# The last mixer's order left to the scheduler, convolution taps at late priority, and attention scores from stacked operands

## The chip, the cores and the metric

The kernel runs on one core of one Trainium2 chip, as one launch. The metric is the device time of that core in microseconds: the median of three runs.

## The reference

Two times two transformer blocks follow each other on 512 tokens of 1024 features, in fp32. Each block is a mixer and a gated feed-forward part, each followed by a residual sum and a layer norm. The four mixers are latent attention, differential attention, a gated convolution with pooling, and the odd mixer, the last. Only the odd mixer concerns the change. It splits one projection of its input into two branches, in outline:

```python
def odd_mixer(x, w_in, forget_b, dw_w, dw_b, cn_g, cn_b, w_out):
    p = x @ w_in                       # q, k, v: 8 heads x 64; 8 forget gates; 2 x 512 for the convolution
    log_f = jax.nn.log_sigmoid(gates + forget_b)
    y_c = forgetting_attention(q, k, v, log_f)
    y_d = conformer_conv(p_conv, dw_w, dw_b, cn_g, cn_b)
    return jnp.concatenate([y_c, y_d], axis=-1) @ w_out
...
    # forgetting_attention, per block of 128 queries
    logits = q . k / sqrt(64) + cum[query] - cum[key]     # cum: running sum of log_f over the tokens
    probs = softmax(causal(logits))
    out = probs @ v
...
    # conformer_conv
    h = p[:512] * sigmoid(p[512:])
    h = causal_dwconv(h, dw_w) + dw_b  # 31 taps for each of 512 channels
    h = silu(layer_norm(h))
```

## The kernel before, in words

Every fp32 operand is held as a high part, cast to the matrix engine's format, and a low part, the difference. A product is three matrix products that add up in PSUM (`mm3`, L370: high x high, high x low, low x high). Weights come from HBM by DMAs that SyncE issues in the order of a list (`weight_plan`). Each tile of 128 rows and 1024 columns is split on arrival: ScalarE casts the high part (`whi`, L170), and VectorE or GpSimd forms the low part (`wlo`, L171). The table `ONPOOL` says which projections go to GpSimd, and `OTHERWISE` lists the tiles by number for which that is turned round.

In the odd mixer (`odd`, L1331) the projections run with the token axis as the free one, 512 columns. Two of four gated units come from the part of the program before it; units 2 and 3 (`glu`) are 48 products of 512 columns each. The values and the forget gates come from one projection of 264 columns (`W.next("od_v", 2, 264)`, 96 products), the other half of the values from `others` (48 products each for two tiles). Queries and keys come in pairs of heads (`pair`): two projections of 24 products a pair.

The convolution is a chain for each of four tiles of channels. A tap on VectorE is a product and a sum in one instruction over 128x512 elements (L1381, first taps L1379). The fourth tile's taps are a product on ScalarE into a temporary tile `tp` (L1386, two buffers) and a sum on GpSimd (L1387).

Log-sigmoid (`log_sigmoid`) is a chain of some 16 short VectorE operations on 128x32 elements with one exponential on ScalarE. `sums` makes the running sums by two products with a triangle and with ones (L1509, L1510), VectorE adds them up, ScalarE casts the high part (`cumh`, L1519), and `spread` writes high and low parts into two tiles `ab` for four heads. `rows` turns these by eight transposes (L1545); this is done for heads 0 to 3 and again for heads 4 to 7. A score block (`score`) of 128 queries is then five products: three of 64 rows (one head's features), one of four rows that adds the difference of the running sums (L1580), and one that adds the causal mask (L1581). VectorE takes the row minimum (L1593), ScalarE the exponential with its sum (L1594), VectorE the reciprocal (L1586), ScalarE the norm (L1590). The blocks are transposed (L1053), split (`pth` L1066, `ptl` L1068) and multiplied with the values (`attend`), and the output is split into `yh` and `yl` (L378, L379).

The order of all this on TensorE, VectorE, ScalarE and GpSimd is that of the code (`by_hand(Pool)`): no scheduler moves anything. `step(taps, us)` issues `us` microseconds' worth of projection products out of a list of generators (`fill`), then the vector work that the step before has left behind (`done`), then so many VectorE taps (`conv`) and GpSimd taps (`conv3`). The table `OD` says how many for each head. The order is: the gated units, the values and gates, queries and keys of the first pair with log-sigmoid and sums between them, then the heads, two deep, with the other projections as fill; then layer norm of the convolution, output projection.

Of the kernel before, what the change touches and what calls it, by code (L numbers as in the profile page):

```python
# [42 lines left out]
for _k, _w in (("g_q", 3), ("g_kv", 2), ("g_sub", 1), ("conv_w", 12), ("pool_s", 4), ("dw_w", 124),  # L43
# [11 lines left out]
OTHERWISE = (11, 12, 15, 20, 23, 24, 25, 73, 79, 80, 81, 82, 83, 84, 85, 86, 88, 90, 91, 100, 102, 103, 224, 226, 231)  # L55
# [5 lines left out]
    "taps": (0.4, 0.9, 0.7, 0.7, 0.9, 0.4, 0.2, 0.2, 1.6),  # L61
    "pool": (0.45, 0.65, 0.55, 0.45, 0.45, 0.35, 0.45, 0.35, 0.45),
    "look": (3, 2, 2, 2, 1, 1, 3, 2, 3),
    "order": 's0 s1 s2 s3 v t0 t1 t2 t3',
    "pre": (2.6, 3.4, 2.2, 2.2),
    "glu": 1.8,
    "v": 2.5,
    "pool0": 0.35,
# [169 lines left out]
def weight_plan(a):  # L238
# [53 lines left out]
    for j in range(4):  # L292
        if j < 2:
            add("od_a", a["od_d"][0, j])
        add("od_g" if j < 2 else "od_x", a["od_d"][1, j])
        if j > 1:
            add("od_x", a["od_d"][0, j])
    for u in range(4):
        add("od_v", a["od_v0"][u])
    for x in "0" + ORDER:  # L300
# [13 lines left out]
def kernel(ctx: ExitStack, tc: tile.TileContext, a: dict, out: bass.AP):  # L314
# [1016 lines left out]
    def odd(xT, open_x, FIRST, names):  # L1331
        with pool("odd") as op_:
# [16 lines left out]


            now, after, due, due3, AHEAD = [], [], [0.0], [0.0], [2]
            POOL_TAPS = [OD["pool0"]]

            def done(*work):

                after.extend(work)

            def step(taps, us=0.0):
                fill.take(us)
                work = list(now)  # L1360
                now[:], after[:] = after, []
                for w in work:
                    w()
                if W.at < W.used + AHEAD[0]:
                    W.prep()
                due[0] += taps
                n = int(due[0])
                due[0] -= n
                conv(n)
                due3[0] += POOL_TAPS[0]  # L1370
                n = int(due3[0])
                due3[0] -= n
                conv3(n)

            def tap(j, k, pool=False):
# [8 lines left out]
                else:  # L1384
                    tp = op_.tile([P, S], F32, name="tp", tag="tp", bufs=2)
# [3 lines left out]
            TAPS = [deque((j, k) for k in range(CONV)) for j in range(4)]  # L1389
            GL, turn_of = set(), deque(range(3))  # L1390

            def conv(n):

                while n > 0:
                    for j in (*turn_of, 3):
                        if j in GL and TAPS[j]:
                            break
                    else:
                        return
                    tap(*TAPS[j].popleft())  # L1400
                    if j < 3:
                        turn_of.remove(j)
                        turn_of.append(j)
                    n -= 1

            def conv3(n):

                while n > 0 and 3 in GL and TAPS[3]:
                    tap(*TAPS[3].popleft(), pool=True)
                    n -= 1  # L1410

            def gate(j, pa, pg):
                nc.scalar.activation(cv[j], pg, AF.Sigmoid)
                nc.vector.tensor_mul(gl[j][:, CONV - 1:], cv[j], pa)
                GL.add(j)
# [7 lines left out]
            def glu(j):  # L1423
                pg = acc()
                yield from steps_T(pg, "od_x")
                done(lambda: nc.scalar.activation(cv[j], pg, AF.Sigmoid))
                pa = acc()
                yield from steps_T(pa, "od_x")

                def times():  # L1430
                    nc.vector.tensor_mul(gl[j][:, CONV - 1:], cv[j], pa)
                    GL.add(j)

                done(times)

            Q, MADE, SCORED = {}, set(), set()

            def pair(p):
                got = []
                while p > 1 and 2 * p - 3 not in SCORED:  # L1440
                    yield None
                for s in range(2):
                    ps = acc()
                    yield from steps_T(ps, ("od_q", "od_k")[s])
                    hi = ov.tile([P, S], F32R, name="qh", tag=f"qh{s}", bufs=2)
                    lo = ov.tile([P, S], F32R, name="ql", tag=f"ql{s}", bufs=2)
                    got += [hi, lo]
                    done(lambda hi=hi, lo=lo, ps=ps, s=s: split(hi, lo, ps, -0.125 if s == 0 else None))
                done(lambda: Q.update({p: got}))
# [19 lines left out]
            def have(p):  # L1469
                fill.until(lambda: p in Q or p in MADE)  # L1470
                while p not in Q:
                    step(1)

            fill = Fill([glu(2), glu(3)])
# [4 lines left out]
            while fill.parts:  # L1479
                step(OD["glu"], 1.3)  # L1480
            fill.parts.extend([pair(0)] + [others() if x == 'v' else pair(int(x)) for x in ORDER])
# [6 lines left out]
            def log_sigmoid():  # L1488
# [4 lines left out]
                conv(2)  # L1493
# [3 lines left out]
                conv(1)  # L1497
# [7 lines left out]
            def sums():  # L1505
# [6 lines left out]
                def add():  # L1512
# [7 lines left out]
                    spread(0)  # L1520
# [7 lines left out]
            ab = [op_.tile([P, NT, 4, 32], F32, name=f"ab{i}", tag=("yh", "yl")[i], bufs=4) for i in range(2)]  # L1528
            for i in range(2):
                nc.gpsimd.memset(ab[i], 0.0)  # L1530
                nc.gpsimd.memset(ab[i][:, :, :, 2 * i:2 * i + 2], 1.0)
            AB = {}

            def spread(g):
                c, h = cum[:, :, 4 * g:4 * g + 4], f32(cumh[:, :, 4 * g:4 * g + 4])
                nc.vector.tensor_copy(ab[1][:, :, :, 0], h)
                nc.vector.tensor_sub(ab[1][:, :, :, 1], c, h)
# [353 lines left out]
```

## Time and profile before

| what | value |
|---|---|
| median of three runs | 2274.2 us (2273.18, 2274.2, 2282.26) |
| profiled execution | 2284.52 us, its span 2282.7 us |
| mean granted clock of TensorE | 0.988 of full speed |
| busy over the whole span | TensorE 97%, VectorE 76%, ScalarE 44%, GpSimd 11% |
| odd mixer's first row minimum (start) | 1748.00 us |
| last head's low half `yl` (start) | 1871.57 us |
| first output product with a convolution half (start) | 1893.96 us |

Times in the rows are from the start of the span. The share of an engine over the whole span says little about the odd mixer, which is a tenth of it; the windows further down cut its stretches out. Durations of successive instructions of an engine overlap a little, so that the distance of their starts is the cost of one in a run of many. TensorE's granted clock stands as a share of its full 2.4 GHz; 0.50 is 1.2 GHz.

### The profile page before, as it was taken

How to read it: one execution, taken by the hardware profiler on the slowest of the kernel's cores; microseconds unless marked ns; L12 is line 12 of the kernel's file. 1: busy time of each engine (PE TensorE's matmuls, PEld its weight loads, DVE VectorE, ACT ScalarE, POOL GpSimd, SP SyncE). 2: the span in 40 equal slices, each digit the busy share in tenths (PEclk: the TensorE clock that was granted, in tenths of full speed). 3: DMA queues.
4: the chain of work that ended last, by engine and by line, in shares of the span. 5: the costliest groups of instructions: out<-in, count | busy, mean ns of one | idle time of the engine just before them, and what ended most of it. 6: DMA issues, size and time to landing. Idle time of an engine off the chain costs nothing. (4 is left out here: it accounts for less than half of the span.)

```text
span 2282.7 us, 35239 instructions
## 1 busy us (share of the span) xinstructions
PE 2223.8 (97%) x14148; PEld 1987.0 (87%) x14148; DVE 1729.6 (76%) x2806; ACT 994.5 (44%) x1665; POOL 246.6 (11%) x195
## 2 busy tenths in 40 slices
PE   8999999999999999999999999999998999999997
PEld 8888999998987789999988899999886768999996
DVE  5777888886666788888675688887766756988886
ACT  4655444433665454433342344343325654443341
POOL 2200000001312100000000000000046521000001
PEclk9999999999999999999999999999998979999999
DMA  5213333333221133233232333333222013333331
GB/s 172 64 47 102 102 112 97 98 93 105 96 67 65 37 120 111 94 111 103 92 107 93 100 104 111 103 93 111 65 88 83 28 38 108 96 107 106 103 100 57
DMA packets 59364, 210.50 MB, mean 92 GB/s; under 512 B 6624, under 2 KB 6880, under 8 KB 59200
## 3 DMA queue, kind: packets, MB, share of 16 engines
q1 hardware_dynamic: 56304, 198.97, 27.7%
q0 software_dynamic: 2320, 8.23, 1.2%
q8 instruction: 111, 1.82, 0.3%
q10 hardware_dynamic: 576, 1.05, 0.1%
q14 instruction: 53, 0.43, 0.1%
HBM read 206.12 MB, written 2.10 MB: 91 GB/s over the span
## 5 line engine op out<-in xcount | busy, mean ns | idle before, releaser
L170 ACT ACTIVATE whi<-wraw 128x1024 fp32r<-128x1024 f32 (+3 forms) x528 | 520.0, 988 | 814.0 <-PE acc L372 481.8
L171 DVE TENSOR_TENSOR wlo<-wraw,whi 128x1024 fp32r<-128x1024 f32 (+2 forms) x475 | 536.8, 1131 | 117.0 <-ACT whi L170 116.0
L371 PE MATMUL acc<-xh,whi 128*128 128x256 f32 (+1 forms) x1712 | 527.7, 308 | 0.4 <-DVE kl L1098 0.4
L372 PE MATMUL acc<-xl,whi 128*128 128x256 f32 (+1 forms) x1712 | 523.7, 306 | 3.1 <-DVE xl L481 3.1
L373 PE MATMUL acc<-xh,wlo 128*128 128x256 f32 (+1 forms) x1712 | 522.9, 306 | 2.9 <-DVE wlo L171 2.9
L372 PEld LDWEIGHTS acc<-xl,whi 128*128 128x128 f32 x1712 | 323.6, 189 | 27.6 <-DVE xl L481 4.3
L371 PEld LDWEIGHTS acc<-xh,whi 128*128 128x128 f32 x1712 | 323.6, 189 | 24.7 <-DVE kl L1098 0.5
L373 PE MATMUL acc<-xs,wlo 128*128 128x256 f32 x1216 | 341.3, 282 | 0.0
L372 PE MATMUL acc<-xql,whi 128*128 128x256 f32 x1216 | 341.0, 281 | 0.0
L373 PEld LDWEIGHTS acc<-xh,wlo 128*128 128x128 f32 x1712 | 323.2, 189 | 19.5 <-DVE wlo L171 3.9
L371 PE MATMUL acc<-xs,whi 128*128 128x256 f32 x1216 | 339.0, 280 | 0.0
L372 PEld LDWEIGHTS acc<-xql,whi 128*128 128x128 f32 x1216 | 228.5, 188 | 5.5
L371 PEld LDWEIGHTS acc<-xs,whi 128*128 128x128 f32 x1216 | 229.6, 189 | 3.5
L373 PEld LDWEIGHTS acc<-xs,wlo 128*128 128x128 f32 x1216 | 228.1, 188 | 0.3
L171 POOL TENSOR_TENSOR wlo<-wraw,whi 128x1024 fp32r<-128x1024 f32 (+2 forms) x53 | 130.4, 2463 | 548.0 <-ACT whi L170 547.6
L389 POOL TENSOR_TENSOR lnr<-lnv,mhalf 128x1 f32<-128x1 f32 x32 | 23.7, 740 | 1264.4 <-DVE lnv L387 1264.4
L371 PE MATMUL tr<-whi,hh 128*128 128x512 f32 (+1 forms) x296 | 117.8, 398 | 0.0
L782 DVE TENSOR_TENSOR sums<-sums,acc 128x512 f32<-128x512 f32 x76 | 52.2, 687 | 85.5 <-PE acc L373 85.0
L372 PE MATMUL tr<-wlo,hh 128*128 128x512 f32 (+1 forms) x296 | 116.8, 395 | 0.0
L373 PE MATMUL tr<-whi,hl 128*128 128x512 f32 (+1 forms) x296 | 115.8, 391 | 0.0
L373 PE MATMUL ps<-whi,hl 128*128 128x512 f32 x288 | 113.7, 395 | 0.0
L371 PE MATMUL ps<-whi,hh 128*128 128x512 f32 x288 | 113.4, 394 | 0.0
(355 smaller groups left out, 4140.5 us busy)
## 6 DMA issues: line engine op xcount, KB each, us to landing
wraw<-in_gu_dram SPq DMA_DIRECT2D x176, 512.0 KB, 3.6
wraw<-in_dn_dram SPq DMA_DIRECT2D x88, 512.0 KB, 3.5
wraw<-in_ev_in_dram SPq DMA_DIRECT2D x16, 512.0 KB, 3.6
wraw<-in_mla_o_dram SPq DMA_DIRECT2D x8, 512.0 KB, 3.7
wraw<-in_df_q_dram SPq DMA_DIRECT2D x8, 512.0 KB, 3.5
wraw<-in_df_k_dram SPq DMA_DIRECT2D x8, 512.0 KB, 3.6
wraw<-in_df_v_dram SPq DMA_DIRECT2D x8, 512.0 KB, 3.6
wraw<-in_df_o_dram SPq DMA_DIRECT2D x8, 512.0 KB, 3.6
```

The lines of the kernel that those rows point to most:

```text
L170: self.nc.scalar.activation(hi, raw[:, o:o + n], AF.Copy)
L171: eng.tensor_sub(lo, raw[:, o:o + n], hi.bitcast(F32))
L371: nc.tensor.matmul(ps, ah, bh, start=first, stop=False)
L372: nc.tensor.matmul(ps, ah, bl, start=False, stop=False)
L373: nc.tensor.matmul(ps, al, bh, start=False, stop=last)
L389: nc.gpsimd.tensor_tensor(r[:, :n], v[:, :n], mhalf[:, :n], op=OP.pow)
L782: nc.vector.tensor_add(g[:, 1:3], g[:, 1:3], v)
```

## The change

The region in which the code's order holds is gone for the odd mixer: the scheduler orders the instructions of all engines by priorities and its own costs. `done` runs its work at once, `step` only issues fill, and the quotas of taps are gone. When a gated unit is there, all 31 taps of its tile are issued with a priority that lies 4000 and more behind (`conv`).

The value and gate projection comes ahead of the gated units 2 and 3 (the weights' list too). The log sums are taken at the sixth step of those units and the bias rows made at the ninth, for all eight heads at once. `tp` has one buffer.

The scores' operands are stacked in tiles of 128 rows, two heads a pair, two pairs in turn: `qa` holds a head's high query part and the bias rows, `qq` its high and low parts, `kb` the high key part and the bias (chosen for the head by `own_rows`), `kk` the low and the high one. A block is two products of 128 rows and the mask.

```diff
-OTHERWISE = (..., 224, 226, 231)
+OTHERWISE = (..., 224, 226, 227)
...
+    "sums": 6,
+    "rows": 9,
+    "late": 4000,
...
             def done(*work):
-
-                after.extend(work)
-
-            def step(taps, us=0.0):
-                fill.take(us)
-                work = list(now)
-                now[:], after[:] = after, []
                 for w in work:
                     w()
+
+            def step(us=0.0):
+                fill.take(us)
                 if W.at < W.used + AHEAD[0]:
                     W.prep()
-                due[0] += taps
...
-                    tp = op_.tile([P, S], F32, name="tp", tag="tp", bufs=2)
+                    tp = op_.tile([P, S], F32, name="tp", tag="tp", bufs=1)
...
+            def conv(j):
+
+                at = tc.cur_priority
+                for k in range(CONV):
+                    tc.cur_priority = at + OD["late"] + 20 * k + 4 * j
+                    tap(j, k, j == 3)
+                tc.cur_priority = at
...
+            STACK = [[[ov.tile([P, S], F32R, name=f"{n}{b}{m}") for n in ("qa", "qq", "kb", "kk")]
+                      for m in range(2)] for b in range(2)]
...
+            def place(p, s, ps):
+
+                every = [(*STACK[p % 2][m], HALF[m], HALF[1 - m]) for m in range(2)]
+                for qa, qq, kb, kk, own, other in every:
+                    nc.scalar.activation((kb if s else qq)[own], ps[own], AF.Copy, scale=1.0 if s else -0.125)
+                for qa, qq, kb, kk, own, other in every:
+                    if s:
+                        nc.vector.tensor_sub(kk[own], ps[own], f32(kb[own]))
+                    else:
+                        nc.vector.scalar_tensor_tensor(qq[other], ps[own], -0.125, f32(qq[own]), op0=OP.mult, op1=OP.subtract)
+                for qa, qq, kb, kk, own, other in every:
+                    nc.scalar.activation(kk[other] if s else qa[own], f32((kb if s else qq)[own]), AF.Copy)
+
+            def bias(p):
+
+                for m in range(2):
+                    h, other = 2 * p + m, HALF[1 - m]
+                    nc.scalar.activation(STACK[p % 2][m][2][other], f32(ROWS["k"][other]), AF.Copy, scale=own_rows[other, h:h + 1])
...
-            region = ExitStack()
-            region.enter_context(by_hand(mybir.EngineType.Pool))
...
-                qh, ql, kh, kl = Q[p]
-                ms = slice(64 * i, 64 * i + 64)
+                qa, qq, kb, kk = Q[h // 2][h % 2]
...
-                mm3(ps[:, :n], qh[ms, qs], ql[ms, qs], kh[ms, :n], kl[ms, :n], True, False)
-                r = slice(32 * (h % 4), 32 * (h % 4) + 4)
-                nc.tensor.matmul(ps[:, :n], AB[h // 4, 0][r, qs], AB[h // 4, 1][r, :n], start=False, stop=False)
+                nc.tensor.matmul(ps[:, :n], qa[:, qs], kb[:, :n], start=True, stop=False)
+                nc.tensor.matmul(ps[:, :n], qq[:, qs], kk[:, :n], start=False, stop=False)
                 nc.tensor.matmul(ps[:, qs], idb, mkb, start=False, stop=True)
...
+            fill.parts.extend([glu(2), glu(3)])
+            n = 0
+            while fill.parts:
+                step(1.3)
+                n += 1
+                if n == 1:
+                    choose()
+                if n == OD["sums"]:
+                    sums()
+                if n == OD["rows"]:
+                    rows()
```

VectorE, in the log-sigmoid (`lf` are its tiles, `cv` the convolution's sums, `gl` the gated units, `sm` the taps' weights); first before, then after:

```order
L1494 TENSOR_SCALAR lf_17226<-lf_17226 128x32
L1495 RECIPROCAL lf_17226<-lf_17226 128x32
L1496 TENSOR_TENSOR lf_17226<-lf_17226 128x32
L1381 SCALAR_TENSOR_TENSOR cv1_17060<-gl1_17056,sm_91,cv1_17060 128x512
L1498 TENSOR_TENSOR lf_17226<-lf_17226 128x32
L1499 TENSOR_SCALAR lf_17226<-lf_17226 128x32
L1501 SCALAR_TENSOR_TENSOR lf_17226<-lf_17226 128x32 x8
L1502 SCALAR_TENSOR_TENSOR lf_17226<-lf_17226 128x32
L1503 SCALAR_TENSOR_TENSOR lf_17226<-lf_17226 128x32
L1381 SCALAR_TENSOR_TENSOR cv2_17061<-gl2_17057,sm_91,cv2_17061 128x512
L1381 SCALAR_TENSOR_TENSOR cv0_17059<-gl0_17055,sm_91,cv0_17059 128x512
```

```order
L1473 RECIPROCAL lf_17151<-lf_17151 128x32
L1363 SCALAR_TENSOR_TENSOR cv0_17059<-gl0_17055,sm_91,cv0_17059 128x512
L1363 SCALAR_TENSOR_TENSOR cv1_17060<-gl1_17056,sm_91,cv1_17060 128x512
L1474 TENSOR_TENSOR lf_17151<-lf_17151 128x32
L1363 SCALAR_TENSOR_TENSOR cv0_17059<-gl0_17055,sm_91,cv0_17059 128x512
L1363 SCALAR_TENSOR_TENSOR cv1_17060<-gl1_17056,sm_91,cv1_17060 128x512
L1475 TENSOR_TENSOR lf_17151<-lf_17151 128x32
L1363 SCALAR_TENSOR_TENSOR cv0_17059<-gl0_17055,sm_91,cv0_17059 128x512
L1363 SCALAR_TENSOR_TENSOR cv1_17060<-gl1_17056,sm_91,cv1_17060 128x512
L1476 TENSOR_SCALAR lf_17151<-lf_17151 128x32
L1381 TENSOR_TENSOR gl2_17057<-cv2_17061,acc_17341 128x512
```

Eleven rows of before hold the log-sigmoid up to its last step but for three taps and one low half of the queries; eleven rows of after hold four of its steps (one reciprocal ahead, two products, one sum) with six taps and a gated unit between them.

TensorE at head 0's first score blocks (`ps` the score banks, `acc` the projections', `rows` the bias rows, `mkb` and `idb` the mask); first before, then after:

```order
L371 MATMUL ps_17538<-qh_17480,qh_17437 128x128
L372 MATMUL ps_17538<-ql_17481,qh_17437 128x128
L373 MATMUL ps_17538<-qh_17480,ql_17438 128x128
L1580 MATMUL ps_17538<-rows_17520,rows_17514 128x128
L1581 LDWEIGHTS idb_17051
L1581 MATMUL ps_17538<-mkb_17053,idb_17051 128x128
L371 MATMUL acc_17482<-xh_16571,whi_17423 128x512
L372 MATMUL acc_17482<-xl_16572,whi_17423 128x512
L373 MATMUL acc_17482<-xh_16571,wlo_17424 128x512
L371 MATMUL ps_17559<-qh_17480,qh_17437 128x256
```

```order
L369 MATMUL acc_18067<-xl_16572,whi_17754 128x512
L370 MATMUL acc_18067<-xh_16571,wlo_17755 128x512
L1569 MATMUL ps_17678<-kb00_17069,qa00_17067 128x128
L1570 MATMUL ps_17678<-kk00_17070,qq00_17068 128x128
L1571 LDWEIGHTS idb_17051
L1571 MATMUL ps_17678<-mkb_17053,idb_17051 128x128
L1569 MATMUL ps_17700<-kb00_17069,qa00_17067 128x256
L1570 MATMUL ps_17700<-kk00_17070,qq00_17068 128x256
L1571 LDWEIGHTS idb_17051
L1571 MATMUL ps_17700<-mkb_17053,idb_17051 128x128
```

The block is five products and then three, and a projection (`acc`) stood between two blocks of before where after the blocks follow each other.

ScalarE at the cast of the log sums' high part (`cumh`; `tp` is the fourth convolution tile's product, `qh` and `kb`, `kk` high parts of queries and keys); first before, then after:

```order
L170 ACTIVATE whi_17423<-wraw_17362 128x1024
L170 ACTIVATE whi_17448<-wraw_17421 128x1024
L1386 ACTIVATE tp_17453<-gl3_17058,sm_91 128x512
L381 ACTIVATE qh_17437<-acc_17373 128x512
L1519 ACTIVATE cumh_17227<-lf_17226 128x32
L170 ACTIVATE whi_17498<-wraw_17446 128x1024
```

```order
L1368 ACTIVATE tp_17519<-gl3_17058,sm_91 128x512
L167 ACTIVATE whi_18073<-wraw_17837 128x1024
L1410 ACTIVATE kb10_17077<-acc_17748 64x512
L1410 ACTIVATE kb11_17081<-acc_17748 64x512
L1368 ACTIVATE tp_17522<-gl3_17058,sm_91 128x512
L1496 ACTIVATE cumh_17152<-lf_17151 128x32
L1417 ACTIVATE kk10_17078<-kb10_17077 64x512
```

Before, one convolution product stands two rows ahead of the cast, with two buffers to go to; after, one stands right ahead of it, with one buffer, which the 20th GpSimd instruction of the mixer (a sum `cv3` of the product before) leaves free.

## Rows read from the trace of the kernel before

**Rows 1.** Windows: length; busy of PE, PEld, DVE, ACT, POOL; clock; DMA share; GB/s.
```profile
1677.70:1748.00 70.30, 59.04 (x289) 48.90 (x287) 57.25 (x95) 19.39 (x30) 34.03 (x18) 0.90 0.24 70
1748.00:1871.60 123.60, 119.68 (x570) 88.80 (x570) 84.43 (x171) 84.07 (x198) 63.01 (x35) 0.88 0.13 37
```

**Rows 2.** Windows within the attention heads.
```profile
1760.00:1840.00 80.00, 78.55 (x409) 58.92 (x408) 60.60 (x118) 55.83 (x132) 45.14 (x27) 0.96 0.09 27
1840.00:1860.00 20.00, 19.51 (x57) 13.31 (x57) 8.72 (x23) 11.52 (x31) 6.48 (x4) 0.50 0.28 79
```

**Rows 3.** Timeline of TensorE: start us, us, instruction, [idle before <-releaser].
```profile
1731.91 0.61 PE L1509 MATMUL ps<-lf,cst 128*128 128x32 f32 x2 [7.82 <-issue]
```

**Rows 4.** Waits, 1677.7 to 1894: total us, times, longest us.
```profile
ACT e L1594 <- DVE sums L1593: 24.2, 15, 5.1
```

**Rows 5.** Timeline of VectorE in the first stretch.
```profile
1679.09 3.07 DVE L1379 TENSOR_SCALAR cv<-gl,sm 128x512 f32<-128x512 f32 x2
...
1704.59 6.70 DVE L1381 SCALAR_TENSOR_TENSOR cv<-gl,sm,cv 128x512 f32<-128x512 f32 x10
...
1719.83 0.42 DVE L379 TENSOR_TENSOR vl<-ps,vh 128x256 fp32r<-128x256 f32 x1 [0.45 <-ACT vh L378]
```

**Rows 6.** Timeline of GpSimd in the first stretch.
```profile
1679.48 2.40 POOL L171 TENSOR_TENSOR wlo<-wraw,whi 128x1024 fp32r<-128x1024 f32 x1 [3.83 <-ACT whi L170]
...
1706.13 8.67 POOL L171 TENSOR_TENSOR wlo<-wraw,whi 128x528 fp32r<-128x528 f32 x2 [8.57 <-ACT whi L170]
...
1719.46 1.29 POOL L1387 TENSOR_TENSOR cv<-cv,tp 128x512 f32<-128x512 f32 x1
```

**Rows 7.** Timeline of TensorE: score products of heads 0, 6 and 7.
```profile
1749.10 0.50 PE L371 MATMUL ps<-qh 64*128 64x512 f32 x1
...
1750.42 0.23 PE L1581 MATMUL ps<-mkb,idb 128*128 128x128 bf16 x1
...
1835.92 0.32 PE L371 MATMUL ps<-qh 64*128 64x128 f32 x1
...
1847.57 0.47 PE L371 MATMUL ps<-qh 64*128 64x128 f32 x1
```

**Rows 8.** Lines of ScalarE, 1748 to 1871.6: count, busy us, mean ns, idle before.
```profile
L1386 ACT ACTIVATE tp<-gl,sm 128x512 f32<-128x512 f32 x26 | 18.8, 722 | 0.0
L1590 ACT ACTIVATE e<-e,sums 128x128 f32<-128x128 f32 (+3 forms) x32 | 17.9, 559 | 7.5 <-DVE sums L1586 7.5
L1594 ACT ACTIVATE e<-ps,sums 128x128 f32<-128x128 f32 (+3 forms) x32 | 16.8, 525 | 24.2 <-DVE sums L1593 24.2
L1066 ACT ACTIVATE pth<-tr 128x256 fp32r<-128x256 f32 (+1 forms) x48 | 14.2, 350 | 5.4 <-PE tr L1053 5.0
L170 ACT ACTIVATE whi<-wraw 128x1024 fp32r<-128x1024 f32 x9 | 9.5, 1057 | 0.0
L1594 ACT ACTIVATION_READ_ACCUMULATOR e<-ps,sums 128x1 f32 x32 | 6.2, 193 | 0.0
L378 ACT ACTIVATE yh<-ps 64x512 fp32r<-64x512 f32 x8 | 4.7, 590 | 5.8 <-PE ps L373 5.6
```

**Rows 9.** Timeline of ScalarE, an accumulator and what follows.
```profile
1749.69 0.19 ACT L1594 ACTIVATION_READ_ACCUMULATOR e<-ps,sums 128x1 f32 x1
1749.79 0.71 ACT L1386 ACTIVATE tp<-gl,sm 128x512 f32<-128x512 f32 x1
```

**Rows 10.** Timelines of VectorE and TensorE at the ends of the stretches.
```profile
1748.00 0.28 DVE L1593 TENSOR_REDUCE sums<-ps 128x1 f32<-128x128 f32 x1
1748.80 0.17 DVE L1586 RECIPROCAL sums<-sums 128x1 f32<-128x1 f32 x1 [0.53 <-ACT e L1594]
...
1871.57 0.69 DVE L379 TENSOR_TENSOR yl<-ps,yh 64x512 fp32r<-64x512 f32 x1
...
1893.72 0.39 PE L373 MATMUL acc<-whi,yl 128*128 128x512 f32 x1
1893.96 0.39 PE L371 MATMUL acc<-whi,vh 128*128 128x512 f32 x1
```

More of the change, by code (lines that the diff above doesn't have):

```diff
@@ L291, in weight_plan @@
     ffn("2", 0)
[L292 to L297, printed above, removed]
+    for j in range(2):
+        add("od_a", a["od_d"][0, j])
+        add("od_g", a["od_d"][1, j])
     for u in range(4):
         add("od_v", a["od_v0"][u])
+    for j in range(2, 4):
+        add("od_x", a["od_d"][1, j])
+        add("od_x", a["od_d"][0, j])
     for x in "0" + ORDER:
@@ L1444, in pair @@
                     yield from steps_T(ps, ("od_q", "od_k")[s])
[L1445 to L1449, printed above, removed]
+                    done(lambda ps=ps, s=s: place(p, s, ps))
+                if p:
+                    done(lambda: bias(p))
+                done(lambda: Q.update({p: STACK[p % 2]}))
                 MADE.add(p)
@@ L1470, in have @@
                 fill.until(lambda: p in Q or p in MADE)
-                while p not in Q:
-                    step(1)
-            fill = Fill([glu(2), glu(3)])
-            region = ExitStack()
-            region.enter_context(by_hand(mybir.EngineType.Pool))
+                assert p in Q
+            fill = Fill([])
             for j in range(2):
                 gate(j, *FIRST[2 * j:2 * j + 2])
-            while fill.parts:
-                step(OD["glu"], 1.3)
-            fill.parts.extend([pair(0)] + [others() if x == 'v' else pair(int(x)) for x in ORDER])
             vh = op_.tile([P, NT, S], F32R, name="vh")
@@ L1548, in rows, with put @@
-                if g == 0:
-                    done(lambda: spread(1))
+                        nc.tensor.transpose(got[i][:, t * P:(t + 1) * P], ab[i][:, t].rearrange("p d h r -> p (d h r)"), ident)
+                def put():
+                    ROWS["k"] = op_.tile([P, S], F32R, name="rows", tag="yh", bufs=4)
+                    nc.scalar.activation(ROWS["k"], got[1], AF.Copy)
+                    for b in range(2):
+                        for m in range(2):
+                            other = HALF[1 - m]
+                            nc.scalar.activation(STACK[b][m][0][other], got[0][other], AF.Copy)
+                        if b == 0:
+                            bias(0)
@@ L1551, in value @@
+                done(put)
             def value(t, ps):
@@ L1594, in soft @@
                     nc.scalar.activation(e, ps[:, :n], AF.Exp, bias=sums[:, 0:1], scale=-1.0, accum_out=sums[:, 1:2])
-                    now.insert(0, norm)
-                done(soft)
+                    norm()
+                soft()
             def turn_e(h, qb):
@@ L1637, in out_w @@
                 return lambda kc: [w[:, kc % 2] for w in OUT[c][kc // 2]]
-            step(1, OD["pre"][0])
-            step(1, OD["pre"][1])
-            sums()
-            step(1, OD["pre"][2])
-            step(1, OD["pre"][3])
+            fill.parts.extend([glu(2), glu(3)])
[9 more added lines that the diff above has]
+                    rows()
+            fill.parts.extend([pair(0)] + [others() if x == 'v' else pair(int(x)) for x in ORDER])
+            while 0 not in MADE:
+                step(1.3)
             have(0)
@@ L1646, in odd @@
             turns.update(acc=turns["acc"][2:], ps=turns["ps"] + turns["acc"][:1], tr=turns["tr"] + turns["acc"][1:2])
-            rows(0)
-            step(1, 1.0)
-            step(1, 1.0)
             C, OUT = [], {}
             for h in range(-1, 8):
-                us, n, POOL_TAPS[0] = (OD[k][h + 1] for k in ("fill", "taps", "pool"))
+                us = OD["fill"][h + 1]
                 AHEAD[0] = OD["look"][h + 1]
```

99 lines of the change are left out of this document (29 added, 70 removed).

## The prediction

> **What bounds the kernel now.** I read the busy times of the last mixer's stretches first [rows 1]: from the end of the first two gated units' projections to the first row minimum of the softmax, and from there to the last head's low half. A third, from there to the first output product that takes a convolution half, ends at 1893.96 [rows 10]. These 216.3 us are all that the change touches: the instructions ahead of 1677.7 us and behind 1893.96 are the same. The middle stretch is TensorE's: 119.7 of 123.6 us busy, and in its best part, the 80 us of [rows 2], TensorE is at 78.6, VectorE at 60.6, ScalarE at 55.8. In the first stretch it is busy 59.0 of 70.3 us and VectorE 57.3: no engine fills it.
>
> The granted clock comes next. It is 0.90 over the first stretch and 0.88 over the middle one [rows 1], 0.50 from 1840 to 1860 [rows 2], where the heads have no projection beside them. At 0.10 of 70.3 and 0.12 of 123.6 some 20 us go to the lower level, and 16 us to idling, the longest 7.8 us ahead of the log-sum product [rows 3]. Some 178 us are work at the full level.
>
> Then the list of waits. The largest that matters is ScalarE's 24.2 us for row minima [rows 4], which themselves wait for TensorE's scores. So in the middle stretch a shorter score block pays at once. In the first stretch what ends last is the chain of gates, log-sigmoid, log sums, bias rows and scores.
>
> Last, single rows of VectorE and GpSimd [rows 5, 6]. Two first taps, 0.5 us each elsewhere, take 3.07 together while GpSimd's low half of 1024 columns runs its 2.40. Ten taps from 1704.59 take 6.70, and of GpSimd's two halves from 1706.13 the first came through only when they were done. From 1679.1 to the end of those ten, 1711.3, VectorE's ten rows hold 37 taps at 0.66, three first taps, two gates and a low half, 27.8 us. GpSimd's three halves in it are 2.40 and, at 528 columns, twice 1.24: 4.9. The sum is 32.7, the stretch 32.2. Instructions with both operands in SBUF run one at a time on these two engines. Against that, GpSimd's tap sum at 1719.46 took 1.29 beside a value half of VectorE at 1719.83 that reads PSUM and took 0.42: no delay to either.
>
> By the Trainium skill (SBUF — State Buffer, "Who interferes with whom") an instruction of VectorE with two SBUF inputs and one of GpSimd that reads SBUF lock each other out for a whole instruction, and one with a single SBUF input does not. The trace agrees with both halves, except that GpSimd's half at 1706.13 was left out through several taps, not one. By the page, the PSUM readers below come off the sum; were it wrong there, the sum below would be 9.3 us longer.
>
> **The change part by part.**
>
> *Scores.* A block had five products (three of 64 rows, one of 4, the mask) and now has three. The four blocks of head 0 took 0.76, 0.90, 1.12 and 1.36 us, 4.14 together; the last runs from 1749.10 to just behind the mask at 1750.42 [rows 7]. Two of five products less is 1.66 us a head. If products of 128 rows follow each other as the output's do (0.24 us for 512 columns [rows 10], half for 256), a head would take some 1.9 and save 2.2. I take 1.6: 13 us for eight heads where TensorE bounds, double at half clock.
>
> *Stacked operands.* For each pair there are 8 half-row casts and copies, and 2 more for the bias, on ScalarE, about 0.59 us each by the 64x512 row [rows 8], and 4 half-row differences on VectorE, 0.69 each [rows 10]. They replace two casts and two differences of 128 rows. ScalarE gets some 24 operations more in all, 14 us. In the first stretch it has room (19.4 of 70.3 busy), in the middle it counts.
>
> *Order of VectorE's work.* This is the largest term. Before, log-sigmoid stands nearly alone, log sums and spread follow, and taps fill what is left. Now VectorE has 75 of its 93 taps between the first gate and the last write of the bias rows, one to three between any two steps of the log-sigmoid. 75 x 0.66 (the row of ten: 0.67) is 49.5. Readers of PSUM: three gates at 0.69, four value halves at 0.42, eight half-row differences at 0.69, 9.3. The 31 small operations (log-sigmoid, sums, spread) at 0.13, somewhat under the reciprocal's 0.17 [rows 10]: 4.0. Together 62.8 us.
>
> *GpSimd.* ScalarE's cast of the log sums stands behind a convolution product that needs the one temporary buffer left (two before). So GpSimd must be through 20 instructions first: 12 low halves of 1024 columns at 2.40 are 28.8, one of 528 at 1.24, 7 tap sums at 1.29 are 9.0: 39.0 us. Locked out of each other the two make 62.8 + 39.0 - 9.3 = 92.5 us, and 101.8 with no overlap. From 1677.7 the bias rows are written at 1770 to 1779. Without any lock it would be 1740.5, VectorE alone.
>
> *Behind it.* TensorE's projections up to there are 96 products of 264 columns, 192 of 512 and 66 of 256, some 64 us at full clock. It is through with them by about 1745, and stands ahead of the log sums and again ahead of the rows, 10 to 15 us each. What is queued behind its wait: 8 transposes (1 us), 30 products of 0.12 and 24 of 0.24, 9.1 us at full clock and 18 at half, then the first scores, for which VectorE, ScalarE and in the end everything waits. VectorE has 14 taps and two value halves ahead of the first minimum, 10.6 us, and about 5 of GpSimd's lie between. First minimum at 1785 (1776 to 1792), where it was 1748.00 [rows 10]: +37 us (+28 to +44).
>
> *Heads.* With most projections behind it the middle stretch holds less for TensorE. Without a fill beside it a head came 11.65 us behind another at half clock (1835.92 to 1847.57 [rows 7]). Less 3.3 for the scores that is 8.35, times 8 is 67; the three projections of queries and keys left in it (72 products of 0.24) are 16.8 us at full clock, 34 at half: 84 to 101. ScalarE cannot go under its own sum, by the rows of the middle stretch [rows 8]: exponentials 16.8, their accumulators 6.2, norms 17.9, transposed copies 14.2, output halves 4.7, 18 tap products at 0.72, 4 weight halves at 1.06, 20 half-row copies at 0.59, 88.8 in all. An instruction there starts 0.1 us before the one ahead of it ends (1749.69 and its 0.19, then 1749.79 [rows 9]); with that off for some 170 of them it is 72. I take 91 us, between 84 and 101, for heads without fill are the nearest rows. Before it was 123.6: -33 (-52 to -23).
>
> *End.* From the last head's low half to the first convolution product it was 22.4 us [rows 10]. The work stays, some output parts have been issued ahead: -1 (-3 to +2).
>
> *Weights.* The value weights come four loads earlier on SP's queue, the gate weights later, and one low half goes to VectorE in place of another. The DMA share is 0.24 and 0.13 [rows 1]: at nothing, hidden by the 11.7 us of value products ahead. With that cover gone it is one low half, 2.4 us.
>
> **Sum.** +37 - 33 - 1 = +3 us on the profiled execution's 2284.5. That one lies 10.3 above the runs' median of 2274.2; from the median, 2277.
>
> **The rivals.**
>
> *Faster A: the first stretch is not bound by one port.* For it: GpSimd's 63.0 us and VectorE's 84.4 went into the 123.6 of the middle stretch, so there is some overlap. Against it: the 32.7 in 32.2 above. The rows would be written at 1740 to 1745, the first minimum come at about 1757 (+9), the heads as above: 9 - 33 - 1 = -25, so 2249.
>
> *Faster B: the heads run at ScalarE's pace.* First minimum at its early bound (+28), the middle at 78 (72 and a start), -46, the end -1: -19, so 2255. For it: at full clock TensorE would need about 34 + 17 = 51 us there. Against it: heads without fill have been granted 0.50 [rows 2].
>
> *Slower: TensorE drops to its lower level ahead of the bias rows and stays there.* With no overlap the rows are written at 1779, TensorE has stood for 25 us or more, its 9.1 us take 18, the first minimum comes at 1792 (+44), the heads take 101 (-23): +21, so 2295. It decides from where VectorE and GpSimd need over 98 us together. For it: the 32.7 in 32.2. Against it: the 1.29 of the tap sum at 1719.46.
>
> *The change doesn't do what it says.* Taps at late priority would stand behind the log sums. By the order 75 of them stand ahead; the forecast has that already.
>
> **How the numbers follow.** A measurement of this kernel can tell 0.5%, 11.4 us, from no change, so the borders are 2262.8 and 2285.6. Forecast 0.42 (its own range 2264 to 2290), slower rival 0.28, faster A 0.12, faster B 0.18. Of the forecast a tenth ends above 2285.6, and a little of faster B above 2262.8: faster 0.29, same 0.39, slower 0.32. The range reaches a little past faster A and the slower rival: 2247 to 2302.
>
> **What would show it.** Right: the first row minimum at 1776 to 1792; TensorE idle for 20 us or more ahead of the bias rows' transposes while VectorE and GpSimd take turns; score blocks of 512 columns under 0.85 us at full clock; heads 9 to 12 us apart. Wrong: a first minimum before 1765 (the port term), heads 15 us apart (TensorE no lighter), or under 9 (ScalarE's pace).

## The result, and the profile after

The changed kernel takes 2293.1 us (median of 6 runs, 2291.1 to 2294.5), the kernel before 2274.6 beside it: a ratio of 1.0071 (1.0052 to 1.0089). It is slower by 18.5 us by these medians, and by 12 to 20 us by the interval of the ratio.

All 70 runs of before on record spread from 2273 to 2285 us, with a median of 2278.2; the six of the change lie within 3.4 us. A second profile of before (the first experiment) shows where two executions of it part, and its stretches are given beside those of the rows.

| stretch | before, shown execution | before, second profile | after |
|---|---|---|---|
| 1677.7 to the first row minimum | 70.3 | 69.4 | 116.3 |
| to the last head's `yl` | 123.6 | 113.8 | 89.0 |
| to the first convolution product | 22.4 | 23.7 | 17.9 |
| first convolution product, start | 1893.96 | 1884.62 | 1900.86 |
| span | 2282.7 | 2273.2 | 2291.3 |

The windows of after answer to [rows 1] and have its columns; the first stretch is cut where the bias rows are written:

```profile
1677.70:1773.70 96.00, 70.78 (x365) 60.10 (x364) 95.50 (x121) 36.84 (x52) 48.02 (x23) 0.84 0.25 77
1773.70:1794.00 20.30, 12.48 (x75) 10.87 (x74) 19.99 (x18) 12.01 (x17) 13.29 (x6) 0.88 0.25 78
1794.00:1883.00 89.00, 74.73 (x384) 58.34 (x384) 49.82 (x138) 76.16 (x194) 32.46 (x22) 0.89 0.06 19
1883.00:1900.90 17.90, 15.95 (x80) 12.86 (x78) 11.11 (x18) 6.13 (x8) 5.82 (x3) 1.00 0.20 63
```

VectorE is busy for 95.5 of the 96.0 us to the bias rows, with GpSimd at 48.0 beside it; TensorE has 70.8. In the heads TensorE fell from 119.7 to 74.7 and ScalarE has the most, 76.2 of 89.0. Two short windows of after, one in either part:

```profile
1740.00:1750.00 10.00, 0.00 (x0) 0.00 (x0) 9.93 (x9) 8.10 (x13) 9.17 (x6) 0.50 0.32 105
1850.00:1860.00 10.00, 9.31 (x58) 7.43 (x58) 6.38 (x20) 9.95 (x29) 3.08 (x4) 1.00 0.00 0
```

In the first TensorE does nothing, its clock is granted at 0.50, and VectorE and GpSimd are both "busy" nearly all the time. In the second the clock is 1.00 and ScalarE has no time left; so it is from 1830 to 1870 (39.6 of 40 us), but not over the whole of the heads (76.2 of 89.0).

TensorE's timeline of after, the product of the log sums, the queries behind the bias rows, a score block of 512 columns, the first convolution product (to be read against [rows 3, 7 and 10]):

```profile
1755.40 0.61 PE L1486 MATMUL ps<-lf,cst 128*128 128x32 f32 x2 [19.71 <-issue]
...
1792.67 0.79 PE L368 MATMUL acc<-xh,whi 128*128 128x512 f32 x1 [7.82 <-DVE vl L376]
...
1847.88 0.48 PE L1569 MATMUL ps<-kb,qa 128*128 128x512 f32 x1
1848.19 0.40 PE L1570 MATMUL ps<-kk,qq 128*128 128x512 f32 x1
1848.43 0.23 PE L1571 MATMUL ps<-mkb,idb 128*128 128x128 bf16 x1
...
1900.86 0.50 PE L368 MATMUL acc<-whi,vh 128*128 128x512 f32 x1 [1.96 <-ACT vh L375]
```

The 7.8 us wait ahead of the log sums has become 19.7, and there is a second one of 7.8 us, for a value half on VectorE. The score block takes 0.59 us, from 1847.88 to 0.04 behind the start of its mask, where that of [rows 7] takes 1.36 by the same count. The products of before between the two rows shown there are

```profile
1749.43 0.40 PE L372 MATMUL ps<-ql,qh 64*128 64x512 f32 x1
1749.67 0.39 PE L373 MATMUL ps<-qh,ql 64*128 64x512 f32 x1
1750.00 0.49 PE L1580 MATMUL ps<-rows 4*128 4x512 f32 x1
```

VectorE's timeline of after, which answers to [rows 5 and 10]: a step of the log-sigmoid, three taps, the last write of the bias rows, the taps in front of a value half, the first minimum, the last `yl`:

```profile
1706.27 2.38 DVE L1472 TENSOR_SCALAR lf<-lf 128x32 f32<-128x32 f32 x1
...
1737.86 7.30 DVE L1363 SCALAR_TENSOR_TENSOR cv<-gl,sm,cv 128x512 f32<-128x512 f32 x3
...
1773.45 0.27 DVE L1523 TENSOR_TENSOR ab<-cumh,lf 128x64 f32<-128x64 f32 x1
...
1777.33 14.69 DVE L1363 SCALAR_TENSOR_TENSOR cv<-gl,sm,cv 128x512 f32<-128x512 f32 x9
1791.93 0.68 DVE L376 TENSOR_TENSOR vl<-acc,vh 128x512 fp32r<-128x512 f32 x1
...
1793.98 0.62 DVE L1583 TENSOR_REDUCE sums<-ps 128x1 f32<-128x128 f32 x2
...
1882.96 0.69 DVE L376 TENSOR_TENSOR yl<-ps,yh 64x512 fp32r<-64x512 f32 x1
```

GpSimd's timeline of after at the first two of them, which answers to [rows 6]:

```profile
1705.99 2.63 POOL L168 TENSOR_TENSOR wlo<-wraw,whi 128x1024 fp32r<-128x1024 f32 x1 [1.95 <-ACT whi L167]
...
1737.86 2.35 POOL L168 TENSOR_TENSOR wlo<-wraw,whi 128x1024 fp32r<-128x1024 f32 x1
1740.16 1.71 POOL L1369 TENSOR_TENSOR cv<-cv,tp 128x512 f32<-128x512 f32 x1
1741.83 2.79 POOL L168 TENSOR_TENSOR wlo<-wraw,whi 128x1024 fp32r<-128x1024 f32 x1
```

Three taps (2.0 us alone) take 7.30 beside two low halves and a tap sum. The step at 1706.27 works on 32 columns and takes 2.38 us: it ends with GpSimd's half, which began 0.28 us before it. The mean tap up to the bias rows is 1067 ns, where ten in a row took 0.67 each [rows 5]:

```profile
L1363 DVE SCALAR_TENSOR_TENSOR cv<-gl,sm,cv 128x512 f32<-128x512 f32 x73 | 75.1, 1067 | 0.3
```

### The profile page after: what moved, and what is told of

It is laid out like the page before. It is cut to its first block, busy times and chain, and to the rows that moved or that the text cites. A ratio compares the mean times of both kernels' runs of the same rounds, so it can differ in the third digit from the quotient of the medians.

```text
span 2291.3 us, 35147 instructions
## 1 busy us (share of the span) xinstructions
PE 2198.8 (96%) x14076; PEld 1974.9 (86%) x14076; DVE 1755.5 (77%) x2813; ACT 1016.7 (44%) x1700; POOL 239.2 (10%) x195
## 5 line engine op out<-in xcount | busy, mean ns | idle before, releaser
L167 ACT ACTIVATE whi<-wraw 128x1024 fp32r<-128x1024 f32 (+2 forms) x528 | 520.8, 989 | 833.4 <-PE acc L369 513.0
L368 PE MATMUL acc<-xh,whi 128*128 128x256 f32 (+1 forms) x1712 | 527.6, 308 | 14.9 <-DVE vl L376 7.8
L386 POOL TENSOR_TENSOR lnr<-lnv,mhalf 128x1 f32<-128x1 f32 x32 | 23.7, 740 | 1271.2 <-DVE lnv L384 1271.1
```

What stands on the lines that cost most here:

```text
L167: self.nc.scalar.activation(hi, raw[:, o:o + n], AF.Copy)
L368: nc.tensor.matmul(ps, ah, bh, start=first, stop=False)
L386: nc.gpsimd.tensor_tensor(r[:, :n], v[:, :n], mhalf[:, :n], op=OP.pow)
```

## The experiments

**The kernel before again**, unchanged.

> The kernel before once more, unchanged, for a second profile of it: its runs fall into two groups, about 2274 and about 2283, and the trace shown is one of the upper group. If the upper group is a matter of the odd mixer's clock, a profile of the lower group shows the same instruction order with a granted clock above 0.88 in the heads (1748 to 1872) and the first convolution product some 9 us earlier than 1893.96. Rival: the difference lies ahead of the odd mixer (before 1677 us), and the mixer's stretches are the same 70.3, 123.6 and 22.4 us.

2274.97 us. Its windows of the heads, and of the 20 us that [rows 2] show:

```profile
1747.10:1860.90 113.80, 109.63 (x570) 81.69 (x570) 84.21 (x171) 83.66 (x198) 62.99 (x35) 0.97 0.14 41
1840.00:1860.00 20.00, 18.07 (x91) 13.09 (x90) 13.06 (x28) 13.49 (x31) 4.95 (x3) 0.95 0.21 56
```

and the first convolution product:

```profile
1884.62 0.40 PE L371 MATMUL acc<-whi,vh 128*128 128x512 f32 x1
```

The order is the same, the clock is 0.97 over the heads and 0.95 where it was 0.50, and the product comes 9.3 us earlier. The two executions are 9.5 us apart in all, and their heads 9.8 (123.6 and 113.8). So the execution on which the prediction's terms rest had inside its heads nearly all of the 10.3 us that lie between it and the median of three. What decides which clock an execution gets was not found.

**One port or a long queue.** GpSimd writes zeros where it formed the low halves of the odd mixer's projections (a part of the result is left out):

```diff
-        eng.tensor_sub(lo, raw[:, o:o + n], hi.bitcast(F32))
+        if eng is self.nc.gpsimd and self.plan[self.at - 1][0] in ("od_x", "od_v", "od_q", "od_k"):
+            eng.memset(lo.bitcast(F32), 0.0)
+        else:
+            eng.tensor_sub(lo, raw[:, o:o + n], hi.bitcast(F32))
```

> The changed kernel, with GpSimd writing zeros in place of the low halves of the odd mixer's projections: a part of the computation is left out, the instruction only writes and reads nothing. It tells the port from VectorE's own queue. One port: the 13 halves of 2.4 us no longer stand in VectorE's way, the bias rows (1773.7) come at 1744 to 1752, where 76 taps and the 62.8 us of VectorE with GpSimd's 9 us of tap sums end, and the time falls by 20 us or more, to 2265 to 2275. Rival, VectorE's queue: the rows stay at 1770 or later and the time above 2285.

2259.7 us (two runs), 0.9928 (0.9907 to 0.9949) of before. GpSimd's lines up to the bias rows, and the last write of them on VectorE:

```profile
L1372 POOL TENSOR_TENSOR cv<-cv,tp 128x512 f32<-128x512 f32 x10 | 15.5, 1550 | 9.4 <-ACT tp L1371 9.4
L169 POOL MEMSET wlo<- 128x1024 f32 x13 | 12.4, 956 | 32.5 <-PE acc L373 24.7 <-PE ps L373 5.9 <-PE ps L372 1.8
```

```profile
1745.64 0.27 DVE L1526 TENSOR_TENSOR ab<-cumh,lf 128x64 f32<-128x64 f32 x1
```

Nine taps in a row, and the two operations of GpSimd that ran beside them:

```profile
1682.62 6.05 DVE L1366 SCALAR_TENSOR_TENSOR cv<-gl,sm,cv 128x512 f32<-128x512 f32 x9
...
1683.87 0.95 POOL L169 MEMSET wlo<- 128x1024 f32 x1 [2.02 <-PE ps L373]
1686.78 0.95 POOL L169 MEMSET wlo<- 128x1024 f32 x1 [1.96 <-PE ps L373]
```

Each tap took 0.67, as alone [rows 5]: an operation that only writes did not hold them up. 76 taps stand ahead of the rows (75 in the change), and these come at 1745.9 in place of 1773.7. The thirteen halves that read thus cost VectorE 28 us, some 2.1 each, with VectorE's queue nearly as it was: the time goes to the port, by which the expectation means that the two engines lock each other out, and not to the length of the queue. The first minimum comes at 1761.9, 32 us earlier, and the time falls by 33, to less than the 2265 to 2275 that were expected. The zeros also go into TensorE's products; what that does to the time was not told apart, but TensorE does not set the rows, for VectorE is busy for 67.4 of the 68.2 us up to them.

**The low halves on VectorE.**

```diff
-ONPOOL = ("od_x", "od_v", "od_q", "od_k", "od_o", "uq_n", "ukv", "df_o", "mla_o")
+ONPOOL = ("od_o", "uq_n", "ukv", "df_o", "mla_o")
-OTHERWISE = (..., 224, 226, 227)
+OTHERWISE = (..., 224, 226)
```

> The changed kernel, with the low halves of the odd mixer's projections on VectorE in place of GpSimd: 13 operations that cost GpSimd 2.4 us cost VectorE about 1.15. One port (my theory): VectorE gets 15 us more and GpSimd 30 us less, their sum falls by 15, so the bias rows are written near 1760 where they were at 1773.6, the first row minimum comes 10 to 15 us earlier than 1794, the time is 2280 to 2285. Rival, VectorE's own queue is what is long: the rows are written some 14 us later, near 1787, and the time is 2303 or more.

2276.6 us, 0.9990 (0.9980 to 0.9999): 16.5 us off the change by giving work to the busier engine. VectorE's lines up to the bias rows:

```profile
L1363 DVE SCALAR_TENSOR_TENSOR cv<-gl,sm,cv 128x512 f32<-128x512 f32 x70 | 61.3, 904 | 0.2
L168 DVE TENSOR_TENSOR wlo<-wraw,whi 128x1024 fp32r<-128x1024 f32 x14 | 18.1, 1291 | 0.1
```

The taps fall from 1067 to 904 ns. The rows came at 1772.0, hardly earlier, against the expectation: the scheduler now put 16 of GpSimd's tap sums ahead where there were 9, and VectorE has 18 us of halves. The first minimum came at 1779.1, 14.9 us earlier: both value halves that stand ahead of it were done by 1764, where in the change they start at 1776.7 and 1791.9:

```profile
1763.28 0.68 DVE L376 TENSOR_TENSOR vl<-acc,vh 128x512 fp32r<-128x512 f32 x1
...
1771.69 0.26 DVE L1523 TENSOR_TENSOR ab<-cumh,lf 128x64 f32<-128x64 f32 x1
...
1779.12 0.28 DVE L1583 TENSOR_REDUCE sums<-ps 128x1 f32<-128x128 f32 x1
```

So the first minimum gained what was expected, in another place, and the time fell by more than the 8 to 13 us that were expected.

**Taps held behind the log sums.** Taps from the 13th on of tiles 0 and 1, and all of tile 2, are queued behind the last spread:

```diff
+                    if SPREAD:
+                        with tc.issue_after(SPREAD[0]):
+                            tap(j, k, j == 3)
+                    else:
+                        tap(j, k, j == 3)
...
-                conv(j)
+                if j == 3 or SPREAD:
+                    conv(j)
+                else:
+                    conv(j, 0, 12)
+                    GATED.append(j)
```

> The changed kernel, with all taps but the first 12 of the tiles 0 and 1 queued behind the spread of the log sums on VectorE: 24 taps ahead of the bias rows in place of 75. If the taps ahead are what makes the rows late, 51 x 0.66 = 34 us go: rows near 1740, the gap before the log sums (19.7 us) gone, first minimum near 1770 (33 taps now lie between rows and first minimum), and since ScalarE rather than VectorE bounds the heads, most of the 24 us stay: 2270 to 2278. Rival, only moved: the taps come back ahead of the first minimum and in the heads (36 there in place of 4), where VectorE and GpSimd exclude each other again, and the time stays at 2288 to 2294.

2277.6 us, 1.0003 (0.9992 to 1.0014), 15.5 us off the change. Rows at 1715.7, 58 us earlier where 34 were expected; first minimum at 1754.9, 39 us earlier; the heads then took 113.0, 24 longer:

```profile
1715.39 0.26 DVE L1533 TENSOR_TENSOR ab<-cumh,lf 128x64 f32<-128x64 f32 x1
```

```profile
1754.90:1867.90 113.00, 95.46 (x526) 76.23 (x526) 91.03 (x175) 88.94 (x212) 55.29 (x33) 0.95 0.11 33
```

VectorE's 91 and GpSimd's 55 us are there now. The taps' place decides the rows, as expected, but three fifths of the first minimum's gain are given back in the heads: the time is in the expected range, and the rival was right on where the taps go.

**Both**, as two edits together.

> Both remedies on the changed kernel: all taps but 24 queued behind the spread of the log sums, and the projections' low halves on VectorE. If each takes away another part of what the port costs, the first minimum comes near 1748 and the heads grow less than with held taps alone (113 us), to about 100: 2260 to 2270, under both kernels. Rival, the work of VectorE is only moved about, 50 taps now lie beside the heads: 2272 to 2280, no better than either remedy.

2265.5 us, 0.9942 (0.9926 to 0.9958): faster than both kernels. The last write of the rows, the first minimum, and the windows about it:

```profile
1716.38 0.27 DVE L1533 TENSOR_TENSOR ab<-cumh,lf 128x64 f32<-128x64 f32 x1
...
1738.34 0.29 DVE L1596 TENSOR_REDUCE sums<-ps 128x1 f32<-128x128 f32 x1
```

```profile
1677.70:1738.30 60.60, 55.88 (x289) 47.30 (x288) 54.78 (x94) 37.02 (x52) 8.87 (x6) 0.96 0.33 105
1738.30:1856.30 118.00, 96.17 (x525) 77.44 (x524) 104.66 (x192) 88.28 (x210) 52.88 (x30) 0.93 0.11 36
```

GpSimd has 8.9 us of the first stretch. The first minimum comes 10 us earlier than was expected, and the heads take 118.0 where about 100 were: they are longer, not shorter, than with held taps alone, and 50 taps are among them where there were 36. With 36 taps ahead of the spread in place of 24:

> The fastest version so far (2265.5) with 36 taps ahead of the log sums' spread in place of 24, so 41 in place of 50 behind the first minimum. Its bias rows were written at 1716.7 and its first minimum came at 1738.3, so 8 us more ahead of the rows should cost nothing there and take 6 us from the heads (118 us long): 2258 to 2264. Rival, the first minimum moves by as much as the heads shorten: 2264 to 2269.

2265.7 us, 0.9941 (0.9919 to 0.9963), no gain: the rows went from 1716.7 to 1728.3, the first minimum from 1738.3 to 1747.0 and the heads from 118.0 to 108.5, the rival.

**The five-product scores in the changed kernel** (`pair`, `score`, `spread` and `rows` of before).

> The changed kernel with the five-product scores of before (operands split as before, bias rows for four heads at a time) under the scheduler, late taps and early log sums as in the change. What the stacked scores are worth in the change: if ScalarE bounds the heads there (it is busy 9.8 of each 10 us from 1830 to 1870), 24 operations less on ScalarE make up for 13 to 20 us more on TensorE, the heads are 85 to 95 us long and the time stays at 2288 to 2296. Rival, TensorE bounds them and the scores save 13 us or more: the time is 2305 or more.

2289.8 us, 1.0049 (1.0032 to 1.0067). The heads:

```profile
1779.30:1879.80 100.50, 99.73 (x501) 73.77 (x500) 54.48 (x140) 71.94 (x185) 44.41 (x27) 0.97 0.10 32
```

They take 100.5 us and TensorE has 99.7 of them. With the stacks they took 89.0: the scores do save 11.5 us there, and TensorE does bound the old ones, so the first expectation had the right time for a wrong reason. The gain is lost ahead of them: the first minimum comes at 1779.3 with the old scores and 14.7 us later with the stacks. The last of the rows are written within a microsecond of the change's, but the old scores make them for four heads at a time, and those that the first minimum needs are there at 1767.7, six us earlier:

```profile
1767.53 0.17 DVE L1495 TENSOR_TENSOR ab<-cumh,lf 128x16 f32<-128x16 f32 x1
...
1777.63 0.68 DVE L376 TENSOR_TENSOR vl<-acc,vh 128x512 fp32r<-128x512 f32 x1
1779.34 1.07 DVE L1549 TENSOR_REDUCE sums<-ps 128x1 f32<-128x128 f32 x3
```

One value half stands between the rows and the first minimum, where the change has two; the other comes at 1794.3. So beside the stacks' copies the earlier rows and the scheduler's order have a part in the 14.7 us; these were not told apart.

**The same in the fastest version.**

> The fastest version so far (24 taps ahead of the log sums' spread, the others queued behind it, low halves on VectorE; 2265.5) with the five-product scores of before. It tells what the stacked scores are worth once the bias rows are early. In the changed kernel the heads took 89.0 us with them and 100.4 without, but the first minimum came 14.7 us later. If that lateness is the jam's and not the stacks', the 11 us come out here: 2272 to 2280. Rival, the stacks' copies cost what the products save: 2262 to 2269.

2276.0 us, 0.9997 (0.9985 to 1.0008), against 2265.5 with the stacks. Where the rows are early the stacked scores, with the rows for all heads at once, are worth 10.5 us.

**The stacked scores in the order by hand**, with one buffer for `tp`, as in the change.

> The kernel before, its order by hand and its taps' quotas as they were, with the stacked scores alone (one buffer for the fourth tile's products, as in the changed kernel). If the score blocks of the middle stretch pay where TensorE bounds (119.7 of 123.6 us busy), 8 x 1.6 = 13 us go from TensorE there and 24 more operations come to ScalarE, which has 40 us of room: 2262 to 2268 against 2274. Rival, ScalarE's additional copies stand in front of exponentials and the single buffer ties ScalarE to GpSimd: 2272 to 2285.

2286.1 us, 1.0030 (1.0020 to 1.0040). The window of the heads and two waits in it:

```profile
1744.40:1871.00 126.60, 99.72 (x517) 78.99 (x515) 89.28 (x176) 100.10 (x225) 62.30 (x37) 0.89 0.12 38
```

```profile
PE ps L1613 <- ACT e L1628: 13.3, 6, 3.8
ACT tp L1386 <- POOL cv L1387: 6.6, 9, 1.7
```

The time lies a microsecond above the rival's range. TensorE had 10 us less work than the 109.6 of the second profile of before, and stood waiting: for exponentials on ScalarE (100.1 us busy, 83.7 in that profile), which in turn waits for GpSimd's sums. **One buffer alone** in the kernel before:

```diff
-                    tp = op_.tile([P, S], F32, name="tp", tag="tp", bufs=2)
+                    tp = op_.tile([P, S], F32, name="tp", tag="tp", bufs=1)
```

> The kernel before with one buffer for the fourth tile's convolution products in place of two, nothing else. The stacked scores by hand cost 8 us where 9 were expected to go; either the single buffer is at fault (ScalarE then waits for GpSimd, 2282 to 2288 here) or the copies for the stacks and the lighter TensorE's clock (then 2273 to 2281 here, as the kernel before).

2287.1 us (2278.6 to 2291.6), 1.0026 (1.0009 to 1.0043). The clock of 1840 to 1860 in its profile:

```profile
1840.00:1860.00 20.00, 17.78 (x66) 12.15 (x67) 11.91 (x32) 14.23 (x36) 9.99 (x5) 0.69 0.20 66
```

With that spread the buffer's price, some 7 us against the runs of before beside it, is not told apart from the clock's. By hand the kernel with stacks and one buffer (1.0030 of before) takes as long as that with one buffer alone (1.0026): the stacks bring no measured gain there.

**The low halves on VectorE in the kernel before.**

> The kernel before, by hand, with the projections' low halves on VectorE in place of GpSimd. If the shared port also costs the kernel before (taps in its heads took 1.06 us against 0.67 alone), it gains, 2266 to 2272; if TensorE bounds its heads (118.7 of 123.6 us busy) VectorE's wait is off the path there and the 1.15 us each come in front of row minima: 2274 to 2285.

2275.7 us, 0.9981 (0.9969 to 0.9993), 4 us off the 2280.2 of the runs of before beside it: less than the gain in the first half of the expectation. TensorE is busy for 117.0 of the 122.3 us of its heads, as the second half has it.

**Units first.** The gated units 2 and 3 ahead of the values again, log sums at the fifth step of the first pair, rows at the seventh.

> The changed kernel with the gated units 2 and 3 ahead of the values and gates again, as before, and the log sums among the first pair's projections. In the order all 93 taps then stand ahead of the bias rows. If what stands ahead of the rows on VectorE decides, they come 12 us or more later than 1773.7, near 1790, the heads have no taps beside them, and the time is 2293 to 2305. Rival, the place of the log sums is nothing: 2290 to 2295 with rows at 1774.

2297.9 us, 1.0095 (1.0078 to 1.0112). The last write of the rows and the first minimum:

```profile
1797.23 0.27 DVE L1523 TENSOR_TENSOR ab<-cumh,lf 128x64 f32<-128x64 f32 x1
...
1803.69 0.29 DVE L1571 TENSOR_REDUCE sums<-ps 128x1 f32<-128x128 f32 x1 [6.20 <-PE ps L1559]
```

All 93 taps are ahead, the rows come 24 us later and the time is 4.8 us longer. Log sums amid the gated units are worth that much to the change, no more. Of the 24 us, 14 are made up before the first minimum, which comes 6.2 us behind the rows and not 20.3, for both value halves now stand ahead of the rows (1773.0 and 1789.2); the heads without taps (to 1888.8) are 3.9 us shorter.

## Where the prediction was right and where wrong, point by point

The forecast was no change, 2277; the time is 2293. That is inside the stated range of 2247 to 2302, but the range takes in every rival, and the forecast's own, 2264 to 2290, does not hold it. By the prediction's own border of 2285.6 the kernel is slower, to which it gave 0.32. The rival "slower" (2295) came near, in part by luck: from the 2284.5 on which its terms stand, its +21 makes 2305, and the 10.3 us that are taken off stand against heads 12 us shorter than its 101.

*The step that failed* is the last: "+3 us on the profiled execution's 2284.5. That one lies 10.3 above the runs' median of 2274.2; from the median, 2277". The heads' term was made against 123.6 us, an execution that was granted 0.50 for 20 of them, and the 10.3 us were then taken off again. Against the second profile of before, near the median of three, the heads are 113.8; with the 91 that were forecast for them the term is -23 and the sum +13, so 2287. Of the 16 us between 2277 and 2293 this step is 10.3; the other 6 or so are the terms below taken together, of which the largest is that up to the first minimum, 9 us more than was forecast. The median of three was itself low: all 70 runs of before have 2278.2.

*The bias rows*: 1770 to 1779 was forecast, 1773.7 came. (In the eleven rows of before that the section on the change shows, three are taps and none is a low half of the queries; the log-sigmoid stood as nearly alone as the prediction has it.) The port and the 75 taps hold, and the run with zeros shows the port alone. The sum of 92.5 us came near the 96.0 that it took, but GpSimd did not hold back the cast of the log sums: it was through with the 20 instructions at 1754.7, and the cast came at 1768.3, 1.9 us behind the last of VectorE's sums. Three more of GpSimd's instructions, 5.9 us, fell in before the rows. Two waits of TensorE of 10 to 15 us each were forecast; one of 19.7 came, ahead of the log sums, and none ahead of the rows.

*From the rows to the first minimum*: 20.3 us where 15 were forecast, so +46.0 in place of +37, beyond its range (+28 to +44). Nine taps took 14.69 us beside 12 us of GpSimd's, where 5 had been put in; TensorE stood for the value half behind them. This wait of 7.8 us was not foreseen.

*The heads*: 89.0 against 91, for another reason, so the agreement is luck. Half clock and TensorE were to bound them; the clock was 0.89 and ScalarE had 76.2 us of them, between the 72 and the 88.8 of its own sum, as in the rival "faster B". The row that the 91 rests on was misread: the 11.65 us between two heads [rows 7] were not all at half clock, for by the trace products of 512 columns take 0.39 to 0.50 us up to 1840.2, in the first four of them, and 0.63 to 0.79 behind it. The score block saved 2.5 us a head by the trace (blocks of 0.21, 0.36, 0.43 and 0.59), above the 1.6 taken and the 2.2 of the bound; the runs give 10.5 us of time for all eight, or 11.5 of the heads' stretch.

*The end*: -4.5 (-1 was forecast, -3 at most), and 1.7 us more behind the first convolution product, where nothing was to change; the clock was 0.83 from 1900 to 1910, and the cause was not followed. 46.0 - 34.6 - 4.5 + 1.7 is 8.6, by which the spans differ.

*The rival "slower"* had the place right, and the low clock ahead of the rows (0.50 from 1740 to 1760). It did not stay low: it was 1.00 from 1765 to 1785 and 0.89 over the heads.

## What to carry to other kernels

Work for a scheduler's gaps is not free where two engines lock each other out: a chain that others wait for then pays for the filler and for the other engine's work. Here giving that other engine's work to the fuller engine, and queueing the filler behind the chain, made the change 27 us faster (2293.1 to 2265.5), where either alone made it 16. And a sum made against one execution may not be moved to the median before it is known in which stretch the difference lies.

## What was not expected of the hardware

The same program in the same order was granted 0.50 or 0.95 in the same 20 us of two executions (1840 to 1860), 9.3 us apart at the end of the mixer.

The step of the log-sigmoid on 32 columns was held to 2.38 us by GpSimd's half, although it reads one tensor only, with a constant. The kernel before has such a step too, beside GpSimd's halves:

```profile
1723.32 5.19 POOL L171 TENSOR_TENSOR wlo<-wraw,whi 128x1024 fp32r<-128x1024 f32 x2 [2.57 <-ACT whi L170]
...
1726.29 2.25 DVE L1499 TENSOR_SCALAR lf<-lf 128x32 f32<-128x32 f32 x1
```

By the Trainium skill (SBUF — State Buffer, "Who interferes with whom") this kind, `tensor_scalar`, is among those that can take the shared ports too, when its operands meet certain conditions; the rows agree. The prediction's sentence on that section leaves this kind out, although the two first taps of [rows 5], 3.07 us beside a half, are of it; its sum does have these steps in, for it takes off only the readers of PSUM.

Two of five products less took 0.77 us off a score block of 512 columns, where two products of 128 rows cost 0.48 by the output projection's starts [rows 10]. The starts in the block of before are 0.33, 0.24, 0.33 and 0.42 us apart, against 0.31 and 0.24 in that of after: the product of four rows alone takes 0.42 to the next start. Why was not looked into.
